# One change to a decoder-trunk kernel: the two ends of the up projection, own buffers for one load of the down projection, and 32 bytes reserved in SBUF

## The chip, the cores and the metric

The kernel runs on one core of a Trainium2 chip. The metric is the device time of one execution in microseconds (us), the median of the runs shown. TensorE (PE) does the matrix products and transposes, VectorE (DVE) and ScalarE (ACT) the elementwise work, GpSimd (POOL) and SyncE (SP) here mostly start transfers between the chip's memory and SBUF, the on-chip memory of 128 partitions from which the engines read. Products are collected in PSUM, in eight banks of 512 float32 columns.

## The reference, cut to what matters

Three sub-layers stand one behind the other, each with a norm ahead of it, a norm behind it and a residual: a mixer (pooling and forgetting attention, joined by gates), attention to 256 memory tokens, and a gated MLP. The change lies in the last, apart from the reserved bytes, which concern all. S is 1024, D_MODEL 1024, D_FF 2816.

```python
def conv_ffn(h, w_up, conv_w, conv_b, w_down):
    z = h @ w_up
    zc = conv_w[2] * z + conv_w[1] * shift_right(z, 1) + conv_w[0] * shift_right(z, 2) + conv_b
    g, u = zc[..., :D_FF], zc[..., D_FF:]
    return (jax.nn.gelu(g, approximate=True) * u) @ w_down
...
        x = x + rms_norm(merged @ w_mix_out[l], mix_post_g[l])
...
        x = x + rms_norm(mem_attention(h, mem_n, w_xq[l], w_xkv[l], w_xo[l]), xa_post_g[l])
        h = rms_norm(x, ffn_pre_g[l])
        x = x + rms_norm(conv_ffn(h, w_up[l], conv_w[l], conv_b[l], w_down[l]), ffn_post_g[l])
```

## The kernel before

**Products of three matmuls.** Every float32 operand is split into a high part (a copy on ACT, rounded to the matmul's type) and a low part (source minus high, on DVE); `split` does both, on L101 and L102. A product is high times high, high times low and low times high. A matmul holds 128x128 of one operand (the stationary one, the second of its two names in the profile) and streams the other (the moving one, the first name) through it, nearly always 512 columns.

**Two sides of SBUF.** Tile pools take their space from the left end or from the right end. On the left lie `const`, `sm` and `ap` (28 slots of 4 KB a partition with tag A, given out by `slot`), on the right, up to the down projection, `hp` (four large operands, `hslot`) and `wp` (split weights), and from then on `dp` (`dslot`). As the program is built, tiles on the left begin at multiples of 64 bytes, and tiles on the right at 32 bytes above a multiple of 64, since the right end of the space given out, 229344, is itself 32 above one.

**Up projection.** For each of 22 pairs of column blocks (j), seven products p1 to p7 (`product_up`, 12 matmuls each, L1105) take the place of eight, on sums of operand blocks. `up_steps` is the order of these 154 products, n its index. Moving operands: b11, b21, t3 and t4 lie in `hp`, t1, t2 and b22 in `ap` slots. Stationary operands rotate through six pairs (`up_ops`): four pairs `wh`/`wl` in `wp` on the right, two `ox` on the left. `z` collects the results (ACT copies and DVE additions out of PSUM); `gate_done` and `pair_done` convolve, apply the gelu, multiply and store.

**Its start.** The tokens' last quarter (q4 = 3) is transposed on PE (`xtrans(3)`, L915) ahead of product n = 4, through PSUM banks that `ring(q=(0, 1))` gives out, two in turn; ACT copies them out (L918, into `xr`). The sums t1 to t4 of quarters 2 and 3 come from the generator `b_sums`; `plan` says after which product which of its steps is written. The t4 step of quarter 2 consists of two DVE operations on `tr` (L1055, L1056) and a split into `t`.

**Its end.** Product 153 is p4 of j = 21. Behind the loop stand the loads (`load`) and the splits (`prepare`) of the first HEAD = 4 steps of the down projection: their raw data goes into the up projection's raw slots (`head_raw`), their operands into the slots of t1 and t2 (`head_ops`).

**Down projection.** Steps (p, k), seven products by eleven k, 12 matmuls each (L1287). `load(i + 4)` and `prepare(i + 2)` are written ahead of `products(i)`. Weights of products other than p1 go through a ring of four buffers, `wd`. For p7, each pair of steps loads two of them, b22 and b12, DVE subtracts the second from the first in place (L1255), and the difference is split.

The loads on SP keep their written order. Otherwise a scheduler of the framework sets the order on each engine, so that the written order is only its starting point.

Of the kernel before, what the change touches and what calls it, by code (L numbers as in the profile page):

```python
# [9 lines left out]
F32 = mybir.dt.float32  # L10
# [6 lines left out]
P = 128  # L17
# [7 lines left out]
NJ = FF // P  # L25
# [13 lines left out]
def hybrid_kernel(ctx, tc, out, x, xT, g_col, mem, gains, b_forget, w_fm, w_v0, w_v1, pool_w, pool_scale,  # L39
                  w_pool_br, w_fox_br, w_mix_out, w_xq, w_xk, w_xv, w_xo, w_up, conv_w, conv_b,  # L40
                  w_down):
    nc = tc.nc
    const = ctx.enter_context(tc.tile_pool(name="const", bufs=1))
    sm = ctx.enter_context(tc.tile_pool(name="sm", bufs=16))
    ap = ctx.enter_context(tc.tile_pool(name="ap", bufs=28))

    front = ctx.enter_context(ExitStack())
    hp = front.enter_context(tc.tile_pool(name="hp", bufs=4, side="right"))
# [26 lines left out]
    def ring(**kinds):  # L75

        rings.clear()
        for k, ids in kinds.items():
            rings[k] = [list(ids), 0]
# [404 lines left out]
    def step(gen, n):  # L484
        for _ in range(n):
            next(gen, None)
# [118 lines left out]
    t1 = [slot(s="t1") for _ in range(8)]  # L605
# [290 lines left out]
    def xtrans(q4, k2s=range(4)):  # L896

        for n in ("b11", "b21"):
            if n not in quarters:
                quarters[n] = hslot(n)  # L900
        if q4 >= 2 and q4 not in raws_b:
            raws_b[q4] = ([slot((P, 4, 256), s="rb") for _ in range(2)] if q4 == 2 else
                          [t.rearrange("p (k n) -> p k n", k=4) for t in xrs[q4]])
        c = slice((q4 % 2) * 256, (q4 % 2) * 256 + 256)
        if q4 < 2:
            def dst(k2):
                o, k = quarters[("b11", "b21")[k2 // 2]], 2 * (k2 % 2)
                return o[:, k:k + 2, c], o[:, 4 + k:6 + k, c]
            transpose_pair(yrs[q4], dst, k2s, g_cols[:, 2])
            return  # L910
        for k2 in k2s:
            b = bank("q").rearrange("p (k t) -> p k t", k=2)
            for kk in range(2):
                for t in range(2):
                    nc.tensor.transpose(b[:, kk, t * P:(t + 1) * P],  # L915
                                        yrs[q4][t][:, (2 * k2 + kk) * P:(2 * k2 + kk + 1) * P], ident)
            for kk in range(2):
                nc.scalar.activation(raws_b[q4][k2 // 2][:, 2 * (k2 % 2) + kk], b[:, kk], AF.Copy,  # L918
                                     scale=g_cols[:, 2, 2 * k2 + kk:2 * k2 + kk + 1])
# [117 lines left out]
    def b_sums(q4):  # L1037

        c = slice((q4 % 2) * 256, (q4 % 2) * 256 + 256)
        r12, r22 = raws_b[q4]  # L1040
        t_ = slot((P, 4, 256), s="tr") if q4 == 2 else g_post.rearrange("p (k n) -> p k n", k=4)
        b11, b21 = quarters["b11"], quarters["b21"]
        nc.vector.tensor_tensor(t_, r12, f32(b11[:, :4, c]), ALU.subtract)
        nc.vector.tensor_tensor(t_, t_, f32(b11[:, 4:, c]), ALU.subtract)
        b_split(q4, "t1", t_)
        yield
        nc.vector.tensor_tensor(t_, r22, t_, ALU.subtract)
        b_split(q4, "t2", t_)
        yield
        b_split(q4, "b22", r22)  # L1050
        yield
        nc.vector.tensor_tensor(r12, r22, r12, ALU.subtract)
        b_split(q4, "t3", r12)
        yield
        nc.vector.tensor_tensor(t_, f32(b21[:, :4, c]), t_, ALU.subtract)  # L1055
        nc.vector.tensor_tensor(t_, t_, f32(b21[:, 4:, c]), ALU.add)  # L1056
        b_split(q4, "t4", t_)
        yield
# [24 lines left out]
    ps = psum.enter_context(tc.tile_pool(name="ps2", bufs=1, space=bass.MemoryType.PSUM, reuse_waits="tile"))  # L1083
    eight = [ps.tile([P, 512], F32, tag=f"c{i}", name=f"acc{i}", bufs=1) for i in range(8)]
    banks[:] = eight[4:]
    ring(q=(0, 1))
    UX, UZ, UY = [eight[i] for i in (6, 0, 2, 7)], [eight[i] for i in (1, 3)], eight[4:6]
    up_raws += yrs[2]
    up_ops += [tuple(o[:, i].rearrange("p k n -> p (k n)") for i in range(2)) for o in ox]
# [7 lines left out]
    def product_up(n):  # L1097
        j, p = up_steps[n]
        o = {"p5": UY[j % 2], "p3": UY[j % 2], "p2": UZ[j % 2]}.get(p, UX[j % 4])
        ah, al = operand_up.pop(n)  # L1100
        bh, bl = b_part(B_OF[p], 0), b_part(B_OF[p], 1)
        for k in range(4):
            ks = slice(k * P, (k + 1) * P)
            for i, (l, r) in enumerate(((ah, bh), (ah, bl), (al, bh))):
                nc.tensor.matmul(o, l[:, ks], r[k // 2][:, k % 2], start=i == k == 0 and p in ("p1", "p5", "p2"),  # L1105
                                 stop=i == 2 and k == 3, skip_group_check=True)
        if p == "p1":
            z[j] = [slot(s="zg"), None]
            nc.scalar.activation(z[j][0][:, left], o, AF.Copy)
        elif p == "p5":  # L1110
            z[j][1] = slot(s="zu")
            nc.scalar.activation(z[j][1][:, right], o, AF.Copy)
        elif p == "p6":
            nc.scalar.activation(z[j][0][:, right], o, AF.Copy)
        elif p == "p3":
            nc.vector.tensor_add(z[j][0][:, right], z[j][0][:, right], o)
        elif p == "p7":
            nc.vector.tensor_add(z[j][1][:, right], z[j][1][:, right], o)
        elif p == "p2":
            nc.vector.tensor_add(z[j][0][:, left], z[j][0][:, left], o)  # L1120
        else:
            nc.scalar.activation(z[j][1][:, left], o, AF.Copy)
# [11 lines left out]
    def gate_done(j):  # L1134
        gates[j] = conv_wide(z[j][0], j)
        nc.scalar.activation(gates[j], gates[j], AF.Gelu_apprx_tanh)

    def pair_done(j):

        d = conv_wide(z[j][1], NJ + j)  # L1140
        nc.vector.tensor_mul(d, d, gates.pop(j))
        nc.gpsimd.dma_start(out=act_d[j], in_=d)
        z.pop(j)
        act_ring[j] = d
        if j % 2:
            s_ = slot((P, 512), s="sd")
            nc.vector.tensor_tensor(s_, act_ring.pop(j - 1)[:, right], act_ring.pop(j)[:, right], ALU.add)
            nc.gpsimd.dma_start(out=sum_d[j // 2], in_=s_)

    sums_b3[3] = b_sums(3)  # L1150

    plan = {0: ((2, 1),), 1: ((2, 1),), 2: ((2, 1),), 3: ((2, 1),), 4: ((3, 1),), 5: ((3, 2),), 6: ((3, 1),), 7: ((3, 1),)}
    done_up = set()
    waiting = []
    for n in range(len(up_steps)):
        j, p = up_steps[n]
        if n == 4:
            xtrans(3)
        product_up(n)
        for q4, m in plan.get(n, ()):  # L1160
            step(sums_b3[q4], m)
        prepare_up()

        while waiting and waiting[0][0] <= n:
            waiting.pop(0)[1]()
        done_up.add((j, p))
        defer = 4 if j < 6 else 0
        for jj in (j - 1, j):
            if (jj, "g") not in done_up and {(jj, "p3"), (jj, "p2")} <= done_up:
                done_up.add((jj, "g"))  # L1170
                waiting.append((n + defer, lambda jj=jj: gate_done(jj)))
        if p == "p4":
            waiting.append((n + defer, lambda j=j: pair_done(j)))

    HEAD = 4
    front.close()  # L1180
    dp = ctx.enter_context(tc.tile_pool(name="dp", bufs=6, side="right", reuse_waits="tile"))

    def dslot(tag, dt=F32, bufs=None):
        return dp.tile([P, 2, 512], dt, tag=tag, name=nm(tag), bufs=bufs)

# [9 lines left out]
    operands = {}  # L1195
    got = {}

    head_raw = [t.rearrange("p (k n) -> p k n", k=2) for t in up_raws[2:]]
    head_ops = [t for n in ("t1", "t2") for half in range(2) for t in b_slots[n, half]]

    LOADS = {"p1": ("a11", "b11"), "p5": ("s", "b12"), "p6": ("b22", "a12"), "p3": ("b22", "a21"),
             "p7": ("b22", "b12"), "p2": ("b21",), "p4": ("a22",)}
# [2 lines left out]
    def load(i):  # L1205

        p, k = steps[i]
        if k % 2:
            return
        n = min(2, NK - k)  # L1210

        def send(out, in_):
            in_order(nc.sync.dma_start(out=out, in_=in_))

        for q in LOADS[p]:
            if q == "s":
                r = dslot("sa")
                for kk in range(n):
                    send(r[:, kk], sum_d[k + kk])
            elif q[0] == "a":  # L1220
                r = head_raw.pop(0) if i < HEAD else slot((P, 2, 512), s=q)
                c = slice((int(q[1]) - 1) * 512, int(q[1]) * 512)
                for kk in range(n):
                    send(r[:, kk], act_d[2 * (k + kk) + int(q[2]) - 1][:, c])
            else:
                r = (dslot("wd", bufs=4) if p != "p1" else head_raw.pop(0) if k < HEAD else
                     dslot("sb"))
                c = slice((int(q[2]) - 1) * 512, int(q[2]) * 512)
                send(r[:, :n], w_pairs[int(q[1]) - 1][:, k:k + n, c])
            got[q if q in ("a11", "a12", "s") else (p, q), k // 2] = r  # L1230
# [45 lines left out]
                    got.pop(((p, q), k2))  # L1276

    accs = {"x": eight[:4], "y": eight[4:]}

    def products(i, ts=range(4)):  # L1280
        p, k = steps[i]
# [56 lines left out]
            eng.dma_start(out=out[tg * P:(tg + 1) * P, ns], in_=xt[:, ns])  # L1338

    AHEAD = 2  # L1340
    for i in range(HEAD):
        load(i)
    for i in range(HEAD):
        prepare(i)
    for i in range(len(steps)):
        p, k = steps[i]
        if i + 2 * AHEAD < len(steps):
# [93 lines left out]
```

## Time and profile before

| | us |
|---|---|
| median of 3 runs | 1515.12 |
| lowest and highest run | 1515.02, 1515.87 |
| the profiled execution | 1518.38 |
| its span | 1516.6 |
| PE busy | 1466.8 |
| DVE busy | 1024.3 |
| ACT busy | 715.8 |

The mean granted clock of the profiled execution is 0.989 of full speed. The span runs from about 0 to 1516.6: the mixer to about 609 us, its output projection to about 700, the attention to 855, the up projection to 1284, the down projection from there. In the timeline rows the first number is the start and the second the length of a group of equal instructions, and the bracket says how long the engine was idle before it and what released it. Successive matmuls overlap by their drain, so that the distance of two starts, not the duration of one, is what a matmul costs in a row of matmuls.

### The profile page before, as it was taken

To read this page: it belongs to the slowest core of one execution; us is meant where nothing else is said; L and a number is where in the kernel's file an instruction comes from. 1 tells how busy PE (TensorE), PEld (TensorE's weight loads), DVE (VectorE), ACT (ScalarE), POOL (GpSimd) and SP (SyncE) were. 2 spreads that over 40 slices of the span, in tenths; PEclk is the share of its full clock that TensorE was granted. 3 is DMA by queue.
4 is the path that set the end of the run, shared out by engine and by line. 5 is a ranking of instruction groups with operands and counts; after the bars stand their busy time and mean duration, and the time that the engine had idled before them with its cause. 6 is when DMAs were issued, how large, how long until landed. Compare 5 with 4: busy or idle time off the path is not lost. (4 is left out here: it accounts for less than half of the span.)

```text
span 1516.6 us, 19098 instructions
## 1 busy us (share of the span) xinstructions
PE 1466.8 (97%) x7052; PEld 1211.5 (80%) x7052; DVE 1024.3 (68%) x1505; ACT 715.8 (47%) x1328; POOL 135.5 (9%) x303
## 2 busy tenths in 40 slices
PE   7999999999999999999999799999999998999996
PEld 7988888778888888877788588888888887888785
DVE  7578787673234344576646789787778876786785
ACT  6355655322222233455668755454444444444362
POOL 4101000000000000042112100000000000000003
PEclk9999999999999999999999899999999999999998
DMA  5254343111111224344412223222222223863542
GB/s 170 70 124 96 81 107 76 43 42 48 50 61 43 84 80 158 110 142 164 139 56 98 97 70 118 91 76 91 91 90 91 91 91 120 287 217 98 185 149 111
DMA packets 62014, 159.49 MB, mean 105 GB/s; under 512 B 7585, under 2 KB 8033, under 8 KB 61921
## 3 DMA queue, kind: packets, MB, share of 16 engines
q1 hardware_dynamic: 49472, 114.20, 25.3%
q0 software_dynamic: 12304, 43.82, 8.0%
q8 instruction: 55, 0.90, 0.3%
q14 instruction: 39, 0.31, 0.1%
q10 hardware_dynamic: 144, 0.26, 0.0%
HBM read 118.50 MB, written 27.16 MB: 96 GB/s over the span
## 5 line engine op out<-in xcount | busy, mean ns | idle before, releaser
L101 ACT ACTIVATE wh<-wr 128x512 fp32r<-128x512 f32 x137 | 85.3, 628 | 225.9 <-PE wide L234 124.1
L1287 PE MATMUL acc<-o,o 128*128 128x512 f32 x828 | 188.9, 390 | 1.8 <-DVE o L102 1.8
L1287 PEld LDWEIGHTS acc<-o,o 128*128 128x128 f32 x828 | 155.1, 188 | 35.5 <-DVE o L102 3.3
L1105 PE MATMUL acc<-t,wh 128*128 128x512 f32 x472 | 147.1, 393 | 0.0
L102 DVE TENSOR_TENSOR wl<-wr,wh 128x512 fp32r<-128x512 f32 x137 | 93.0, 686 | 61.1 <-ACT wh L101 61.0
L1105 PE MATMUL acc<-b,wh 128*128 128x512 f32 x360 | 111.8, 392 | 0.0
L1105 PEld LDWEIGHTS acc<-t,wh 128*128 128x128 f32 x472 | 88.6, 188 | 20.1
L1105 PE MATMUL acc<-t,wl 128*128 128x512 f32 x236 | 92.7, 393 | 0.0
L1105 PE MATMUL acc<-t,ox 128*128 128x512 f32 x348 | 84.0, 393 | 0.0
L236 PE MATMUL wide<-h,wl 128*128 128x512 f32 x256 | 79.5, 390 | 1.0 <-DVE wl L102 1.0
L232 PE MATMUL wide<-h,wh 128*128 128x512 f32 x256 | 79.5, 391 | 0.5 <-ACT wh L101 0.3
L1105 PEld LDWEIGHTS acc<-b,wh 128*128 128x128 f32 x360 | 67.5, 188 | 14.8
L234 PE MATMUL wide<-h,wh 128*128 128x512 f32 x256 | 79.1, 390 | 0.0
L163 PE MATMUL bank<-h,wh 128*128 128x512 f32 x192 | 77.0, 401 | 1.5 <-DVE qk L441 1.5
L101 ACT ACTIVATE wh<-su 128x512 fp32r<-128x512 f32 x59 | 37.1, 630 | 86.5 <-DVE su L1008 52.4
L1105 PEld LDWEIGHTS acc<-t,ox 128*128 128x128 f32 x348 | 65.3, 188 | 15.1
L164 PE MATMUL bank<-h,wh 128*128 128x512 f32 x192 | 75.9, 396 | 0.0
L165 PE MATMUL bank<-h,wl 128*128 128x512 f32 x192 | 75.7, 394 | 0.0
L1105 PE MATMUL acc<-b,wl 128*128 128x512 f32 x180 | 70.5, 392 | 0.0
L1105 PE MATMUL acc<-b,ox 128*128 128x512 f32 x252 | 63.7, 404 | 0.0
L613 DVE TENSOR_TENSOR sg<-wide,r1b 128x1024 f32<-128x1024 f32 x16 | 19.6, 1224 | 62.7 <-PE wide L236 62.7
L102 DVE TENSOR_TENSOR pt<-bank,pt 128x512 fp32r<-128x512 f32 (+2 forms) x96 | 50.9, 551 | 11.0 <-ACT pt L101 10.7
(387 smaller groups left out, 3545.2 us busy)
## 6 DMA issues: line engine op xcount, KB each, us to landing
wd<-in_w_down SPq DMA_DIRECT2D x30, 512.0 KB
wr<-in_w_fm SPq DMA_DIRECT2D x28, 512.0 KB
act<-d POOLq DMA_DIRECT2D x22, 512.0 KB, 2.9
a<-act SPq DMA_DIRECT2D x40, 256.0 KB
wr<-in_w_mix_out SPq DMA_DIRECT2D x16, 512.0 KB
wr<-in_w_up SPq DMA_DIRECT2D x16, 512.0 KB
ur<-in_w_up SPq DMA_DIRECT2D x14, 512.0 KB
y<-in_w_up SPq DMA_DIRECT2D x14, 512.0 KB
```

What stands on the lines that cost most here:

```text
L101: nc.scalar.activation(hi, src, AF.Copy)
L102: nc.vector.tensor_tensor(lo, src, f32(hi), ALU.subtract)
L163: nc.tensor.matmul(o, lh, rh, start=start, stop=False)
L164: nc.tensor.matmul(o, lh, rl, start=False, stop=False)
L165: nc.tensor.matmul(o, ll, rh, start=False, stop=stop)
L232: nc.tensor.matmul(o[h], wh[:, ks], hT[h][0][:, k], start=st, stop=False)
L234: nc.tensor.matmul(o[h], wh[:, ks], hT[h][1][:, k], start=False, stop=False)
L236: nc.tensor.matmul(o[h], wl[:, ks], hT[h][0][:, k], start=False, stop=sp)
L613: nc.vector.tensor_mul(sg, og, r1b)
L1105: nc.tensor.matmul(o, l[:, ks], r[k // 2][:, k % 2], start=i == k == 0 and p in ("p1", "p5", "p2"), stop=i == 2 and k == 3, skip_group_che ...
L1287: nc.tensor.matmul(o, oa[:, l, tt], ob[:, r], start=n == k == 0 and p in ("p1", "p5", "p2"), stop=n == 2 and k == NK - 1, skip_group_check ...
```

## The change

Four things are done.

- A tile of 32 bytes a partition is taken from the right end first, and zeroed by one POOL instruction. As built, all tiles of the right pools that a matmul reads then begin at multiples of 64 bytes, as on the left.
- At the start of the up projection the transposes' ring has three banks, (3, 0, 1), and the t4 step of quarter 2 is written after product 7 and no longer after product 3.
- At its end the loads of the first four down steps are written after p3 of j = 21, and their splits after p7 (steps 0 and 1) and p2 (steps 2 and 3); the gate and the convolutions of j = 21 go to the list `later`, from which the down projection takes one entry a step.
- The b12 tiles of p7 get `ap` slots of their own (`wd7`) instead of buffers of the ring `wd`.

```diff
     ap = ctx.enter_context(tc.tile_pool(name="ap", bufs=28))
+
+    pad = ctx.enter_context(tc.tile_pool(name="pad", bufs=1, side="right"))
+    nc.gpsimd.memset(pad.tile([P, 8], F32, name="pad"), 0.0)
...
-    ring(q=(0, 1))
+    ring(q=(3, 0, 1))
...
-    plan = {0: ((2, 1),), 1: ((2, 1),), 2: ((2, 1),), 3: ((2, 1),), 4: ((3, 1),), 5: ((3, 2),), 6: ((3, 1),), 7: ((3, 1),)}
+    plan = {0: ((2, 1),), 1: ((2, 1),), 2: ((2, 1),), 4: ((3, 1),), 5: ((3, 2),), 6: ((3, 1),), 7: ((2, 1), (3, 1))}
...
         product_up(n)
+        if (j, p) == (NJ - 1, "p3"):
+            head_raw += [t.rearrange("p (k n) -> p k n", k=2) for t in up_raws[2:]]
+            head_ops += [t for n_ in ("t1", "t2") for half in range(2) for t in b_slots[n_, half]]
+            for i in range(HEAD):
+                load(i)
+        for i in {"p7": (0, 1), "p2": (2, 3)}.get(p, ()) if j == NJ - 1 else ():
+            prepare(i)
...
-        defer = 4 if j < 6 else 0
+        defer = 4 if j < 6 else 0 if j < NJ - 1 else 99
...
-                r = (dslot("wd", bufs=4) if p != "p1" else head_raw.pop(0) if k < HEAD else
+                r = (dslot("wd", bufs=4) if (p, q) not in (("p1", "b11"), ("p7", "b12")) else
+                     slot((P, 2, 512), s="wd7") if p == "p7" else head_raw.pop(0) if k < HEAD else
                      dslot("sb"))
...
-    for i in range(HEAD):
-        load(i)
-    for i in range(HEAD):
-        prepare(i)
```

Apart from these lines, definitions move ahead of the loop, and line numbers shift: up to about L1150 a line of before is three further down in the changed kernel.

**ACT at the start of the up projection.** The rows begin with the copy of product n = 3's result. `t_853` before and `t_855` afterwards are the operand t4, `tr` its source, `xr` the transposed last quarter. Before:

```order
L1109 ACTIVATE zg_7230<-acc_7127 128x512
L101 ACTIVATE t_853_7255<-tr_7090 128x2x256 x2
L918 ACTIVATE xr_7000<-acc_7131,g_cols 128x256 x2
L918 ACTIVATE xr_7000<-acc_7132,g_cols 128x256 x2
L918 ACTIVATE xr_7001<-acc_7131,g_cols 128x256 x2
L101 ACTIVATE b_847_7208<-xr_7001 128x2x256
L918 ACTIVATE xr_7001<-acc_7132,g_cols 128x256 x2
```

Afterwards:

```order
L1112 ACTIVATE zg_7235<-acc_7132 128x512
L104 ACTIVATE t_855_7369<-tr_7095 128x2x256 x2
L921 ACTIVATE xr_7005<-acc_7139,g_cols 128x256 x2
L921 ACTIVATE xr_7005<-acc_7136,g_cols 128x256 x2
L921 ACTIVATE xr_7006<-acc_7137,g_cols 128x256 x2
L921 ACTIVATE xr_7006<-acc_7139,g_cols 128x256 x2
L104 ACTIVATE b_847_7213<-xr_7006 128x2x256
```

The split of t4 stays ahead of the first copy of a transposed block; the four pairs of copies now stand together, and three banks take the place of two.

**DVE at the same place.** `wl_6080` before, `wl_6085` afterwards, is the low part of a stationary operand of product n = 7. Before:

```order
L1120 TENSOR_TENSOR zg_7182<-zg_7182,acc_7128 128x512
L102 TENSOR_TENSOR b_849_7210<-rb_7059,b_847_7208 128x2x256
L1055 TENSOR_TENSOR tr_7090<-b_775_6688,tr_7090 128x1024
L102 TENSOR_TENSOR b_850_7211<-rb_7059,b_848_7209 128x2x256
L1056 TENSOR_TENSOR tr_7090<-tr_7090,b_775_6688 128x1024
L102 TENSOR_TENSOR wl_6080<-y_6786,wh_6079 128x512
L102 TENSOR_TENSOR t_853_7255<-tr_7090,t_853_7255 128x2x256
```

Afterwards:

```order
L1123 TENSOR_TENSOR zg_7187<-zg_7187,acc_7133 128x512
L105 TENSOR_TENSOR b_849_7215<-rb_7064,b_847_7213 128x2x256
L105 TENSOR_TENSOR wl_6085<-y_6791,wh_6084 128x512
L105 TENSOR_TENSOR b_850_7216<-rb_7064,b_848_7214 128x2x256
L1058 TENSOR_TENSOR tr_7095<-b_775_6693,tr_7095 128x1024
L1059 TENSOR_TENSOR tr_7095<-tr_7095,b_775_6693 128x1024
L1123 TENSOR_TENSOR zg_7235<-zg_7235,acc_7135 128x512
```

The low part `wl` moved from behind the two operations on `tr` to a place ahead of them.

**ACT at the end of the up projection.** `ur` and `y` are the raw slots with the first down operands, `t_832` to `t_835` and `t_843` to `t_846` the operand slots, `zu` and `zg` copies out of PSUM. Before:

```order
L1122 ACTIVATE zu_9781<-acc_7133 128x512
L1136 ACTIVATE d_9873<-d_9873 128x1024
L1112 ACTIVATE zu_9906<-acc_7132 128x512
L1127 ACTIVATE d_9910<-zu_9781,cbt,cwt 128x1024
L1114 ACTIVATE zg_9868<-acc_7127 128x512
L1127 ACTIVATE d_9983<-zg_9868,cbt,cwt 128x1024
L1122 ACTIVATE zu_9906<-acc_7127 128x512
L1136 ACTIVATE d_9983<-d_9983 128x1024
L101 ACTIVATE t_832_7093<-ur_6987 128x512
L101 ACTIVATE t_834_7095<-ur_6987 128x512
```

Afterwards:

```order
L1125 ACTIVATE zu_9786<-acc_7138 128x512
L104 ACTIVATE t_832_7098<-ur_6992 128x512
L104 ACTIVATE t_834_7100<-ur_6992 128x512
L104 ACTIVATE t_835_7101<-ur_6994 128x512
L104 ACTIVATE t_833_7099<-ur_6994 128x512
L1139 ACTIVATE d_9878<-d_9878 128x1024
L1115 ACTIVATE zu_9911<-acc_7137 128x512
L1130 ACTIVATE d_9915<-zu_9786,cbt,cwt 128x1024
L1117 ACTIVATE zg_9873<-acc_7132 128x512
L104 ACTIVATE t_843_7190<-y_6790 128x512
L104 ACTIVATE t_844_7191<-y_6791 128x512
L104 ACTIVATE t_845_7192<-y_6790 128x512
```

Four splits now stand ahead of a gelu and of the copy of p5's result (`zu_9911`), four more (three are shown) ahead of the copy of p4's, which was row seven before.

**PE at the same place**, the last rows of the up projection and the first of the down projection. Before:

```order
L1105 MATMUL acc0_7127<-t4_853_7255,wh_692_6083 128x512 x2
L1105 MATMUL acc0_7127<-t4_853_7255,wl_693_6084 128x512
L1287 MATMUL acc0_7127<-t1_833_7094,t1_832_7093 128x512 x3
L1287 MATMUL acc1_7128<-t1_833_7094,t1_832_7093 128x512 x3
L1287 MATMUL acc2_7129<-t1_833_7094,t1_832_7093 128x512 x3
L1287 MATMUL acc3_7130<-t1_833_7094,t1_832_7093 128x512 x3
```

Afterwards:

```order
L1108 MATMUL acc0_7132<-t4_855_7369,wh_692_6088 128x512 x2
L1108 MATMUL acc0_7132<-t4_855_7369,wl_693_6089 128x512
L1298 MATMUL acc1_7133<-t1_833_7099,t1_832_7098 128x512 x3
L1298 MATMUL acc2_7134<-t1_833_7099,t1_832_7098 128x512
L1298 MATMUL acc0_7132<-t1_833_7099,t1_832_7098 128x512 x3
L1298 MATMUL acc2_7134<-t1_833_7099,t1_832_7098 128x512 x2
L1298 MATMUL acc3_7135<-t1_833_7099,t1_832_7098 128x512 x3
```

Four matmuls of the first down step moved ahead of those into bank acc0, from which p4's result has to be copied first.

**SP at p7's loads**, with the semaphores that each load waits for. Before:

```order
L1213 DMA wd_10890<-in_w_down 128x2x512 [waits DMAHW2_49,DVE_49]
L1213 DMA wd_10892<-in_w_down 128x2x512 [waits DMAHW3_49,DVE_49]
L1213 DMA wd_10932<-in_w_down 128x2x512 [waits DMAHW4_49,DMAHW3_49,DVE_49]
L1213 DMA wd_10934<-in_w_down 128x2x512 [waits DMAHW5_49,DVE_49]
L1213 DMA wd_10973<-in_w_down 128x2x512 [waits DMAHW6_49,DMAHW0_49,DVE_49]
```

Afterwards:

```order
L1187 DMA wd_10895<-in_w_down 128x2x512 [waits DMAHW2_49,DVE_49]
L1187 DMA wd_1084_10897<-in_w_down 128x2x512 [waits DMAHW3_49]
L1187 DMA wd_10937<-in_w_down 128x2x512 [waits DMAHW4_49,DVE_49]
L1187 DMA wd_1090_10939<-in_w_down 128x2x512 [waits DMAHW5_49]
L1187 DMA wd_10978<-in_w_down 128x2x512 [waits DMAHW6_49,DVE_49]
```

The order of the loads is the same; every second one (`wd_1084`, `wd_1090`) no longer waits for DVE.

## Rows read from the trace of the kernel before

**Rows 1.** The page, part 1: busy time, share, instructions of each engine

```profile
PE 1466.8 (97%) x7052; PEld 1211.5 (80%) x7052; DVE 1024.3 (68%) x1505; ACT 715.8 (47%) x1328; POOL 135.5 (9%) x303
```

**Rows 2.** PE's waits, whole span: line, releaser, total us, times, longest

```profile
PE acc L915 <- ACT xr L918: 7.4, 1, 7.4
...
PE acc L1287 <- ACT t L101: 4.7, 1, 4.7
```

**Rows 3.** Windows: us, busy of PE, PEld, DVE, ACT, POOL, clock, DMA share, GB/s

```profile
610.00:660.00 50.00, 50.00 (x216) 40.18 (x215) 29.93 (x47) 25.90 (x53) 2.47 (x7) 1.00 0.28 93
...
1320.00:1370.00 50.00, 50.00 (x222) 41.42 (x221) 43.68 (x57) 25.08 (x45) 0.00 (x0) 1.00 0.61 204
```

**Rows 4.** Timeline of PE, up projection: start, length, engine, line, operation, tiles, count

```profile
968.74 5.75 PE L1105 MATMUL acc<-b,ox 128*128 128x512 f32 x24
...
1267.15 5.63 PE L1105 MATMUL acc<-t,ox 128*128 128x512 f32 x24
1272.62 0.62 PE L1105 MATMUL acc<-b,wh 128*128 128x512 f32 x2
...
1274.71 0.63 PE L1105 MATMUL acc<-b,wh 128*128 128x512 f32 x2
```

**Rows 5.** Timeline of PE at the start of the up projection

```profile
865.60 1.12 PE L915 MATMUL acc<-ident,y 128*128 128x128 f32 x4 [7.38 <-ACT xr L918]
```

**Rows 6.** Timeline of ACT at the same place

```profile
863.67 1.15 ACT L101 ACTIVATE t<-tr 128x512 fp32r<-128x512 f32 x2 [2.87 <-DVE tr L1056]
864.73 1.55 ACT L918 ACTIVATE xr<-acc,g_cols 128x256 f32<-128x256 f32 x4
```

**Rows 7.** Timeline of DVE at the same place

```profile
862.42 1.22 DVE L1056 TENSOR_TENSOR tr<-tr,b 128x1024 f32<-128x1024 f32 x1
863.55 0.68 DVE L102 TENSOR_TENSOR wl<-y,wh 128x512 fp32r<-128x512 f32 x1
```

**Rows 8.** Window behind that wait, columns as in rows 3

```profile
868.00:872.00 4.00, 4.00 (x12) 3.24 (x12) 3.29 (x5) 2.52 (x6) 0.00 (x0) 0.56 0.00 0
```

**Rows 9.** Timeline of PE where the up projection ends

```profile
1283.35 0.39 PE L1105 MATMUL acc<-t,wl 128*128 128x512 f32 x1
1288.42 14.40 PE L1287 MATMUL acc<-t,t 128*128 128x512 f32 x48 [4.68 <-ACT t L101]
1302.67 1.54 PE L1287 MATMUL acc<-o,o 128*128 128x512 f32 x6
```

**Rows 10.** Timeline of ACT there

```profile
1267.70 0.58 ACT L1122 ACTIVATE zu<-acc 128x512 f32<-128x512 f32 x1
...
1270.81 0.58 ACT L1112 ACTIVATE zu<-acc 128x512 f32<-128x512 f32 x1
...
1283.78 0.60 ACT L1122 ACTIVATE zu<-acc 128x512 f32<-128x512 f32 x1 [0.75 <-PE acc L1105]
...
1286.72 2.17 ACT L101 ACTIVATE t<-ur 128x512 fp32r<-128x512 f32 x4
```

**Rows 11.** Windows there: before the wait on ACT, and behind it

```profile
1268.00:1284.00 16.00, 15.74 (x70) 12.61 (x68) 9.06 (x10) 5.02 (x7) 0.53 (x1) 1.00 0.27 98
...
1290.00:1292.00 2.00, 2.00 (x6) 1.56 (x5) 1.88 (x3) 2.00 (x4) 0.00 (x0) 0.50 0.99 376
```

**Rows 12.** Timeline of PE in p7 of the down projection

```profile
1417.64 13.93 PE L1287 MATMUL acc<-o,o 128*128 128x512 f32 x60 [0.32 <-DVE o L102]
1431.90 5.74 PE L1287 MATMUL acc<-o,o 128*128 128x512 f32 x24 [0.33 <-DVE o L102]
1438.78 11.54 PE L1287 MATMUL acc<-o,o 128*128 128x512 f32 x49 [1.14 <-DVE o L102]
```

**Rows 13.** DVE's waits from 1380 to 1450, columns as in rows 2

```profile
DVE wd L1255 <- DMA wd<-in_w_down: 8.8, 6, 2.1
```

**Rows 14.** Timeline of PE in the mixer's attention, scores of one block

```profile
121.77 0.39 PE L458 MATMUL wide<-kd,qs 128*128 128x512 f32 x1
...
122.47 0.40 PE L459 MATMUL wide<-ke,qe 68*128 68x512 f32 x1
```

More of the change, by code (lines that the diff above doesn't have):

```diff
@@ L1148, in pair_done @@
             nc.gpsimd.dma_start(out=sum_d[j // 2], in_=s_)
-    sums_b3[3] = b_sums(3)
-    plan = {0: ((2, 1),), 1: ((2, 1),), 2: ((2, 1),), 3: ((2, 1),), 4: ((3, 1),), 5: ((3, 2),), 6: ((3, 1),), 7: ((3, 1),)}
[L1153 to L1166, printed above, removed]
-        defer = 4 if j < 6 else 0
[L1168 to L1173, printed above, removed]
     HEAD = 4
-    front.close()
-    dp = ctx.enter_context(tc.tile_pool(name="dp", bufs=6, side="right", reuse_waits="tile"))
     def dslot(tag, dt=F32, bufs=None):
@@ L1196, in hybrid_kernel @@
     got = {}
-    head_raw = [t.rearrange("p (k n) -> p k n", k=2) for t in up_raws[2:]]
-    head_ops = [t for n in ("t1", "t2") for half in range(2) for t in b_slots[n, half]]
+    head_raw, head_ops = [], []
     LOADS = {"p1": ("a11", "b11"), "p5": ("s", "b12"), "p6": ("b22", "a12"), "p3": ("b22", "a21"),
@@ L1278, in hybrid_kernel @@
     accs = {"x": eight[:4], "y": eight[4:]}
+    sums_b3[3] = b_sums(3)
+    plan = {0: ((2, 1),), 1: ((2, 1),), 2: ((2, 1),), 4: ((3, 1),), 5: ((3, 2),), 6: ((3, 1),), 7: ((2, 1), (3, 1))}
+    done_up = set()
+    waiting = []
+    for n in range(len(up_steps)):
+        j, p = up_steps[n]
+        if n == 4:
+            xtrans(3)
+        product_up(n)
+        if (j, p) == (NJ - 1, "p3"):
[5 more added lines that the diff above has]
+            prepare(i)
+        for q4, m in plan.get(n, ()):
+            step(sums_b3[q4], m)
+        prepare_up()
+        while waiting and waiting[0][0] <= n:
+            waiting.pop(0)[1]()
+        done_up.add((j, p))
+        defer = 4 if j < 6 else 0 if j < NJ - 1 else 99
+        for jj in (j - 1, j):
+            if (jj, "g") not in done_up and {(jj, "p3"), (jj, "p2")} <= done_up:
+                done_up.add((jj, "g"))
+                waiting.append((n + defer, lambda jj=jj: gate_done(jj)))
+        if p == "p4":
+            waiting.append((n + defer, lambda j=j: pair_done(j)))
+    front.close()
+    dp = ctx.enter_context(tc.tile_pool(name="dp", bufs=6, side="right", reuse_waits="tile"))
     def products(i, ts=range(4)):
```

## The prediction

> **What bounds the kernel now.** First the page's busy times: PE works 1466.8 of 1516.6 us [rows 1], so the time is PE's idle time, 49.8 us, and what a matmul costs while PE is busy. Second PE's waits: the longest single one, 7.4 us on ACT's `xr`, stands at the start of the up projection, and one of 4.7 us on ACT's `t` at its end [rows 2]. Third, how fast a busy PE works. Two stretches of 50 us, both without idle time and at clock 1.00, hold 216 and 222 matmuls of 512 columns [rows 3]. A stretch counts each that touches it, so its length and one matmul's 0.39 us, divided by the count, is the distance of two starts: 50.39/216 = 233 ns and 50.39/222 = 227 ns. That is 2.8% with the same instruction.
>
> What distinguishes them is where the operands lie. The first stretch streams split weights from the right (`wh`, `wl`) against tiles on the left, the second has both on the right. In the up projection, 24 `b,ox` (moving from the right, stationary on the left) take 5.75 us, (5.75 - 0.39)/23 = 233 ns from start to start; 24 `t,ox`, both on the left, take 1272.62 - 1267.15 = 5.47 us, 228 each; behind them nine `b,wh` and `b,wl`, `b` being b22 on the left and `wh` on the right, take 1274.71 - 1272.62 = 2.09 us, 232 each [rows 4]. So both on one side is fast, on either side, and one on each is slow, in either direction. I read this as alignment: right tiles begin 32 bytes above a multiple of 64, left tiles at one. A boundary of some SBUF half does not fit as well: left tiles lie on both sides of the middle of the space and behave alike.
>
> **The change part by part**, against the profiled execution's 1518.4 us.
>
> *The 32 bytes.* I went through all matmuls of 512 columns, took the addresses of the moving tile and of the next stationary one (the one that is loaded meanwhile) from the built program, and the distance of starts from the trace. 2044 undisturbed pairs are mixed (the `b,ox` and `b,wh` of [rows 4] are among the last), by 6.3 ns over 227.0 on average, which is also the difference in [rows 3]: 2044 x 6.3 = 12.9 us. Some 2.6 us of it lie ahead of 540, 2.9 in 540 to 700, 1.8 in 700 to 850, 5.5 in the up projection, nothing in the down projection. The pad makes all of them equal. Where PE waits for others soon after, some of the gain is eaten: ahead of the 7.4 us wait PE's own results feed ACT and DVE, so a chain that starts earlier also ends earlier, and I take off only 0.6. Term **-12.3**. Bounds: -14.5, if the some 80 pairs left out as disturbed and the slow matmuls just behind a change of side gain as well; 0, if alignment is not the cause. POOL's added instruction is its first, and nobody there waits for it.
>
> A page of the Trainium skill speaks against this: "TensorE: Matmul & The Clock Gate", section "Step-by-step: what each phase is for", says that PE has two independent read ports, so that loading the next weights takes no SBUF bandwidth from the running matmul. By it the place of the stationary tile could not matter, the pad's term would be nothing, and the sum that of the second rival below. The trace does not agree as it stands, 233 against 227 ns by where the next stationary tile lies; but that it is the address's last six bits, and not the side, no run here shows yet.
>
> *The start.* PE resumes at 865.60 [rows 5] when ACT has made its first copy into `xr`. ACT did not wait for PE's transposes there but stood behind the split of t4, which waited 2.87 us for DVE's L1056 [rows 6]; DVE ended that at 863.64 [rows 7]. Writing that split behind product 7 should take it out of the way; the order as built shows that it does not: t4's split still stands ahead of all `xr` copies. Worse, `wl`, 0.68 us long [rows 7], moves from behind L1056 to ahead of it, so that L1056 and with it PE's wait end some 0.7 later. For it: three banks let PE do 12 of the 16 transposes ahead of the wait and not 8, so four fewer stand behind it; four there took 1.12 us, a product's first matmul beside them [rows 5]. PE runs at half clock behind the wait, 0.56 in 868 to 872 [rows 8], as it will again. Set row against row, the end of product n = 4 comes 0.3 later, and 0.1 is added for a stationary operand of a later product (n = 11) whose low part is ready that much after it is wanted. Term **+0.4**; bounds -1 (the four transposes for nothing and `wl` hidden, 1.12 at most) and +1.5 (`wl` twice over, 1.36).
>
> *The end.* Before, PE ends its last up matmul's turn at 1283.35 + 0.23, starts again at 1288.42, and does the next 48 matmuls in 14.25 us until 1302.67 [rows 9], most of them at half clock, 0.50 in 1290 to 1292 [rows 11]. The loads had long come; the splits waited behind p4's evacuation and a gelu on ACT, 1283.78 to 1286.72 [rows 10]. Afterwards four splits stand right behind ACT's copy of 1267.70, where ACT is idle for 11 of 16 us [rows 11]; they wait until p5 has read t1 (its 12 matmuls end at about 1269.9) and take 2.17 us [rows 10], until 1271.0. DVE's eight low parts, 0.68 each [rows 7], 5.4 us, go into 6.9 idle us of the same stretch [rows 11]. So PE goes on: 48 x 0.227 = 10.9 us from 1283.58, to 1294.5 and not 1302.7: **-8.2** (4.8 of idle time, 3.4 of half clock). Its cover is thin at two places. The copy of p5 (L1112, before at 1270.81) comes behind splits and gelu at some 1272.5, and p3 wants to add into that bank at 1272.62 [rows 4]; it may cost 0 to 0.3. And p4's copy ends at 1284.38 [rows 10], when PE has done four matmuls into other banks, 1283.58 + 0.91 = 1284.49. If either misses, it costs tenths; if both do and the second step's splits are late too, 2 us: bounds -8.6 and -6. The gate of j = 21, which is late instead, feeds only loads for the last k.
>
> *p7's own buffers.* PE waits 0.32, 0.33 and 1.14 us for DVE's `o` [rows 12], DVE 8.8 us in six times for loads into `wd` [rows 13], and those loads wait until DVE has freed the ring. From 1417.64 to 1438.78 PE needs 21.14 us for 84 matmuls, 84 x 0.227 = 19.07; with the 0.32 ahead that is 2.4 too many. Afterwards every second load waits for no DVE, and the ring holds twice as many steps of the others. Term **-2.3**; bounds -2.7, and +0.5, if earlier weights hold up a load behind them on SP, one of the waits in [rows 12] doubled.
>
> Sum: 1518.4 - 12.3 + 0.4 - 8.2 - 2.3 = 1496.0. The profiled execution lies 3.3 above the median of 1515.12, so the forecast is **1492.7**.
>
> **The rivals.**
> Half of the alignment gain is eaten: what PE gains ahead of 855 (2.6 + 2.9 + 1.8 = 7.3) goes into its waits there. For it: 49.8 us of idle time, most of it ahead of the up projection. Against it: those waits follow from PE's own earlier results. 1492.7 + 6.7 = 1499.4.
> Alignment is not the cause, and left and right differ by their place in SBUF: the pad moves tiles by 32 bytes and no more, and gives nothing. 1492.7 + 12.3 = **1505.0**. For it: in before, side and alignment go together in every pair. Against it: mixed pairs are slow in both directions, and left tiles behave alike wherever they lie.
> Slower: not equality is fast but the 32-byte offset, and the 2803 pairs with both on the right, fast now, become as slow as mixed ones, while mixed ones stay: 2803 x 6.3 = 17.7 in the place of -12.3, 1492.7 + 30.0 = 1522.7. For it: in the mixer's attention scores, with all operands on the left, three distances take 0.70 us, 233 ns each [rows 14]. Against it: the `t,ox` at 228 [rows 4], also on the left, and that those scores stand in groups of four between waits. It turns the sign once equal pairs cost over 231 ns after the change (10.1 us of other terms over 2803 pairs is 3.6 ns above 227).
> The change does not do what it says: at the start that is the forecast already; at the end it would be the splits staying behind the gelu, +8.2, 1500.9; the order as built speaks against it.
>
> **How the numbers follow.** Forecast 0.70; eaten 0.08; no alignment 0.15; slower 0.03; the end's gain missing 0.04. The forecast's own bounds are 1518.4 - 3.3 - 14.5 - 8.6 - 2.7 - 1.0 = 1488.3 and, with the milder ends (-10 for the pad), about 1499. The range 1488.5 to 1505.5 takes in the eaten gain, the missing end and half of "no alignment", about 0.83 in all. A measurement of this kernel tells 0.2%, 3 us, from no change. All cases but one lie below 1512: faster 0.95, within 0.015, slower 0.035.
>
> **What would show it.** Pad: 24 `b,ox` in 5.45 us, 222 matmuls in 50 us of the mixer's output projection. Start: PE's wait on `xr` still there, 7 to 8 us. End: no wait on `t`, clock 1.00 through 1284 to 1300. p7: DVE's wait at its subtraction under 3 us. Wrong would be a mixed pair still at 233 ns, or PE idle for over 1 us at the end of the up projection.

## The result and the profile after

The changed kernel takes 1498.01 us (median of 4 runs, 1495.82 to 1499.68) against 1515.30: ratio 0.9885, 95% interval 0.9867 to 0.9902, faster by 17.3 us. Forecast were 1492.7, 5.3 lower than measured, and a range of 1488.5 to 1505.5. Two later series of the same kernel, each beside the kernel before, gave 1492.51 (0.9859, interval 0.9839 to 0.9878) and 1496.96 (0.9873, 0.9857 to 0.9890); one of the four executions of the first series was disturbed (3747.86 us) and is left out. The profiled execution took 1495.82 us, 22.6 less than that of before; the sum of the terms was 22.4.

The page, part 1, of the changed kernel, and below it PE's waits (line, releaser, total us, times, longest):

```profile
PE 1449.2 (97%) x7052; PEld 1209.0 (81%) x7052; DVE 1022.6 (68%) x1505; ACT 714.1 (48%) x1328; POOL 134.9 (9%) x304
```

```profile
PE acc L918 <- ACT xr L921: 7.9, 1, 7.9
...
PE acc L1298 <- DVE o L105: 0.4, 1, 0.4
```

PE's busy time fell by 17.6 us from [rows 1] with the same 7052 instructions: most of the gain is that the same work takes less time. Of the waits of [rows 2], the one on `t` at the end of the up projection is gone, the one on `xr` is there still and 0.5 longer.

Windows of the changed kernel, columns as in [rows 3]; the first stretch is the one that held 216 matmuls before:

```profile
610.00:660.00 50.00, 50.00 (x222) 41.44 (x221) 31.33 (x47) 27.01 (x54) 5.34 (x10) 1.00 0.32 105
1300.00:1350.00 50.00, 50.00 (x222) 41.42 (x221) 44.24 (x58) 24.51 (x44) 0.00 (x0) 1.00 0.59 200
```

Both stretches now hold 222. PE's timeline in the up projection and at its end:

```profile
961.07 5.60 PE L1108 MATMUL acc<-b,ox 128*128 128x512 f32 x24
...
1254.83 5.60 PE L1108 MATMUL acc<-t,ox 128*128 128x512 f32 x24
1260.27 0.62 PE L1108 MATMUL acc<-b,wh 128*128 128x512 f32 x2
...
1262.31 0.62 PE L1108 MATMUL acc<-b,wh 128*128 128x512 f32 x2
...
1271.15 11.13 PE L1298 MATMUL acc<-t,t 128*128 128x512 f32 x48
1282.11 23.06 PE L1298 MATMUL acc<-o,o 128*128 128x512 f32 x101
```

The 24 `b,ox` of [rows 4] took 5.75 us and take 5.60, (5.60 - 0.39)/23 = 226.5 ns each (the prediction's sign, 5.45, is 24 distances and leaves out that this length holds 23 and one matmul's 0.39, together 5.61); the nine matmuls between the two `b,wh` rows take 2.04 us and not 2.09. Behind the up projection there is no idle time and no half clock: 48 matmuls in 10.96 us, where [rows 9] had 4.68 of idle time and 14.25.

ACT there, with its eight splits in idle time (`ur` and `y` are the raw slots):

```profile
1255.86 2.18 ACT L104 ACTIVATE t<-ur 128x512 fp32r<-128x512 f32 x4
...
1258.89 0.58 ACT L1115 ACTIVATE zu<-acc 128x512 f32<-128x512 f32 x1
...
1260.98 2.19 ACT L104 ACTIVATE t<-y 128x512 fp32r<-128x512 f32 x4
1271.35 0.60 ACT L1125 ACTIVATE zu<-acc 128x512 f32<-128x512 f32 x1 [8.18 <-PE acc L1108]
```

Both thin covers held: p5's copy (L1115) ends at some 1259.5, and p3 starts at 1260.27; p4's copy ends by 1271.95, and PE comes to its bank after four matmuls, at 1271.15 + 0.91.

### The profile page after: what moved, and what is told of

Read it like the earlier page. It is cut to its first block, busy times and chain, and to the rows that moved or that the text cites. A ratio compares the mean times of both kernels' runs of the same rounds, so it can differ in the third digit from the quotient of the medians.

```text
span 1493.7 us, 19105 instructions
## 1 busy us (share of the span) xinstructions
PE 1449.2 (97%) x7052; PEld 1209.0 (81%) x7052; DVE 1022.6 (68%) x1505; ACT 714.1 (48%) x1328; POOL 134.9 (9%) x304
## 4 chain that ended last, share of the span: by engine, by line
PE 83%; DVE 5%; DMA 5%; ACT 2%; issue 2%; POOL 2%; SPq 0%; DVEq 0%; ACTq 0%; POOLq 0%
PE acc L1108 28%; PE acc L1298 10%; PE bank L166 6%; PE bank L167 6%; PE bank L168 6%; PE wide L235 4%; PE wide L239 4%; PE wide L237 4%; PE bank L557 3%; PE wide L166 3%; PE wide L167 3%; PE wide L168 2%; DMA wd<-in_w_down 2%; PE bank L546 2%; DVE o L105 1%
```

## The experiments

The table sets every profiled kernel against the profiled execution of before, in us, by stretches of PE's matmuls in their order, counted from 0 to 7051: ahead of the first up product (0 to 4250), the wait and product n = 4 (4316 to 4346), the up projection behind it (4346 to 6010), its end (6010 to 6160), and from the middle of p7 to the last matmul (6610 to 7051). What lies between stays within 0.3.

| kernel | ahead | start | up | end | p7 on | all |
|---|---|---|---|---|---|---|
| changed | -5.4 | -0.9 | -6.2 | -8.3 | -2.2 | -22.9 |
| changed, again (e9) | -4.6 | -0.6 | -6.2 | -8.3 | -0.3 | -19.8 |
| pad only (e1) | -5.9 | -0.6 | -6.3 | -0.7 | -1.1 | -14.4 |
| no pad (e2) | -1.0 | -0.4 | 0.0 | -8.1 | -0.9 | -10.4 |
| left end too (e3) | -7.3 | -0.4 | -6.2 | -0.5 | -0.9 | -15.4 |
| left 64 lower (e4) | -2.9 | -1.0 | -0.9 | -8.1 | -2.3 | -14.8 |
| left 128 lower (e8) | -3.7 | 0.5 | 0.0 | -8.1 | -2.7 | -14.0 |
| left 256 lower (e12) | -6.5 | 0.5 | -6.2 | -8.3 | 0.4 | -20.1 |
| start undone (e10) | -6.2 | -0.8 | -6.2 | -8.3 | -2.6 | -24.0 |
| ring for p7 (e11) | -5.8 | 0.5 | -6.2 | -8.3 | -0.1 | -19.9 |
| late t4 (e6) | -7.7 | -4.7 | -4.6 | -8.3 | -1.6 | -26.7 |
| late t4, p2 own (e7) | -8.0 | -4.6 | -4.7 | -8.3 | -1.4 | -27.0 |

### Is it alignment?

e1 is the kernel before with the pad alone:

```diff
+    pad = ctx.enter_context(tc.tile_pool(name="pad", bufs=1, side="right"))
+    nc.gpsimd.memset(pad.tile([P, 8], F32, name="pad"), 0.0)
```

> The kernel before with the 32 bytes at the right end and nothing else of the change. Theory A (a matmul of 512 columns costs 227 ns where its moving tile and the next stationary tile begin at the same address modulo 64, and 233 where they don't): 11 to 12 us faster, about 1503.8; the 24 b,ox at 227 ns; the three waits of the start, the end and p7 unchanged. Theory B (left and right side of SBUF, not alignment): no change, 1515.3, the 24 b,ox still at 233.

1504.28 us, ratio 0.9916 (0.9902 to 0.9930): 12.6 faster.

e2 is the changed kernel with these two lines taken out.

> The changed kernel without the 32 bytes. Theory A: what the three other edits give alone, by the changed kernel's trace 8.3 (end) + 2.2 (p7) + 0.7 (start) = 11.2, so about 1504; mixed pairs back at 233 ns. Theory B: as the changed kernel, 1498.

1506.29 us, 0.9931 (0.9916 to 0.9946): 10.6 faster, 2.3 slower than expected, mixed pairs at 233 ns again.

e3 leaves the right end alone and shifts the left:

```diff
+    padl = ctx.enter_context(tc.tile_pool(name="padl", bufs=1))
+    nc.gpsimd.memset(padl.tile([P, 8], F32, name="padl"), 0.0)
     const = ctx.enter_context(tc.tile_pool(name="const", bufs=1))
```

> The kernel before with 32 bytes taken at the left end in the place of the right: all operands of both sides begin 32 above a multiple of 64. Theory A (equal remainders): the same gain as with 32 bytes on the right, 11 to 12 us, about 1503.8. Theory C (multiples of 64 are fast for themselves): nothing gained, and the 2803 pairs with both on the right stay at 227, those on the left get slower, 1515 to 1518. Theory B: 1515.3.

1503.52 us, 0.9911 (0.9898 to 0.9925): the same gain, with everything 32 bytes off a multiple of 64.

e4, e8 and e12 are the changed kernel with the left pools' large tiles lower by 64, 128 and 256 bytes, by smaller constants (e4) and by fewer buffers for the smallest tiles:

```diff
-        return sm.tile([P, cols], F32, tag=f"s{cols}", name=nm(s))
+        return sm.tile([P, cols], F32, tag=f"s{cols}", name=nm(s), bufs=12)
```

This is e12; e8 has it for one of the two sizes. PE, DVE and ACT have the changed kernel's order in both.

> The changed kernel with the left pools' tiles 64 bytes lower (three small constants share two tiles): left and right are equal modulo 64 and differ by 64 modulo 128. If the granule is 64 bytes: as the changed kernel, 1498, mixed pairs at 227. If it is 128 bytes: the 11.6 us are lost again, about 1509.6, mixed pairs at 233.

> The changed kernel with the left pools' big tiles 128 bytes lower (twelve instead of sixteen buffers for the smallest tiles): left and right equal modulo 128, differing by 128 modulo 256. If 128 bytes is the granule: mixed pairs at 227 ns, about 1498. If it is 256 or more: 230 to 233 ns in mixed pairs, as with 64 bytes, about 1506.

> The changed kernel with the left pools' big tiles 256 bytes lower (twelve buffers for both sizes of smallest tiles): equal modulo 256, different modulo 512. Differences of 32, 64 and 128 bytes gave 233 ns in mixed pairs; if the granule is 256 bytes, 227 and about 1496; if it is 512, the length of one row of a stationary tile, 230 to 233 and about 1505.

1505.94 (0.9926, 0.9911 to 0.9941) for 64 bytes; one execution each for 128, 1504.72, and 256, 1498.60. The same group of 24 `b,ox` (right moving, left stationary) in PE's timelines of e2, e3, e4, e8 and e12, in this order:

```profile
967.47 5.75 PE L1105 MATMUL acc<-b,ox 128*128 128x512 f32 x24
```

```profile
959.44 5.60 PE L1107 MATMUL acc<-b,ox 128*128 128x512 f32 x24
```

```profile
964.97 5.66 PE L1109 MATMUL acc<-b,ox 128*128 128x512 f32 x24
```

```profile
965.58 5.75 PE L1108 MATMUL acc<-b,ox 128*128 128x512 f32 x24
```

```profile
961.18 5.60 PE L1108 MATMUL acc<-b,ox 128*128 128x512 f32 x24
```

Equality is what counts, not the multiple (e3 is as fast as e1), and equality modulo 256 bytes: with a difference of 32 (e2) or 128 (e8) a matmul costs 233 ns, with 64 (e4) 229 to 233, by the pair, and 256 (e12) costs nothing. The column "up" says the same over 1664 matmuls: -6.2 or -6.3 in every kernel with equal remainders (but e6 and e7, which wait there, see below), 0.0 with 32 and 128, -0.9 with 64. The rival by which the pad gives nothing falls, and so does the slower one: the pairs on the right stay at 227. The four scores of [rows 14], 233 ns apart before, lie 237 apart in the changed kernel:

```profile
122.15 0.39 PE L461 MATMUL wide<-kd,qs 128*128 128x512 f32 x1
...
122.86 0.40 PE L462 MATMUL wide<-ke,qe 68*128 68x512 f32 x1
```

So they were no evidence on the offset. What slows them was not tried, nor which of the two stationary tiles beside a matmul, its own or the next, has to match. The trace of before says something on the second at the ends of up products (from n = 12 on), where the two lie on different sides. With moving and own tile on one side and the next on the other, a matmul takes 235 ns (23 cases); with moving and next on the right and its own on the left, 229 to 230 (13). That speaks for the next one; but with moving and next on the left and its own on the right it takes 236 (10), so that it stays open.

### The start

e9 is the changed kernel once more, e10 has the old ring and the old plan:

```diff
-    ring(q=(3, 0, 1))
+    ring(q=(0, 1))
...
-    plan = {0: ((2, 1),), 1: ((2, 1),), 2: ((2, 1),), 4: ((3, 1),), 5: ((3, 2),), 6: ((3, 1),), 7: ((2, 1), (3, 1))}
+    plan = {0: ((2, 1),), 1: ((2, 1),), 2: ((2, 1),), 3: ((2, 1),), 4: ((3, 1),), 5: ((3, 2),), 6: ((3, 1),), 7: ((3, 1),)}
```

> The changed kernel once more, for a second profile beside the next two. Expected: median 1493 to 1498; 227 ns in mixed pairs; no wait of PE at the end of the up projection. At its start PE's wait of 7.9 us on xr again, but the time at half clock behind it anywhere from 2.9 us (first profile) to 5.6 us (the run with left tiles 128 bytes lower, whose instructions stand in the same order).

> The changed kernel with the ring of two banks and the old plan for the sums. If the start's edit has a gain of its own: product n = 4 ends 0.7 us later against the matmuls ahead of it than in the changed kernel, and 0.7 in the median. If the 0.7 of the first profile was the clock coming back earlier in that execution: PE resumes some 0.8 us after fewer transposes as forecast (wait 7.2 to 7.5), and the end of n = 4 differs from the changed kernel's by what its time at half clock differs by; the medians within 1 us of each other.

e10 took 1495.62 us (0.9871, 0.9856 to 0.9886), e9 1496.96: no difference beyond the intervals. PE at this place in the changed kernel, in e10 and in e11, which has the changed kernel's order here:

```profile
861.15 1.12 PE L918 MATMUL acc<-ident,y 128*128 128x128 f32 x4 [7.91 <-ACT xr L921]
861.92 6.47 PE L1108 MATMUL acc<-b,ox 128*128 128x512 f32 x23
```

```profile
859.58 1.12 PE L918 MATMUL acc<-ident,y 128*128 128x128 f32 x4 [7.38 <-ACT xr L921]
```

```profile
860.56 1.12 PE L918 MATMUL acc<-ident,y 128*128 128x128 f32 x4 [7.91 <-ACT xr L921]
861.33 7.95 PE L1108 MATMUL acc<-b,ox 128*128 128x512 f32 x23
```

The same 23 matmuls take 6.47 us in one execution and 7.95 in the other. The clock (last column but two) says why; windows of the changed kernel, then of e11:

```profile
860.00:864.00 4.00, 2.85 (x9) 2.46 (x10) 3.29 (x4) 4.00 (x11) 0.00 (x0) 0.50 0.00 0
864.00:868.00 4.00, 4.00 (x18) 3.26 (x18) 3.30 (x6) 2.08 (x4) 0.00 (x0) 1.00 0.00 0
```

```profile
860.00:864.00 4.00, 3.44 (x10) 2.91 (x11) 3.28 (x4) 3.95 (x11) 0.00 (x0) 0.50 0.00 0
864.00:868.00 4.00, 4.00 (x14) 3.14 (x13) 2.00 (x4) 1.54 (x3) 0.00 (x0) 0.68 0.00 0
```

PE resumes 0.6 us later in the changed kernel, and yet is at full clock by 864, while in e11 the half clock goes on past it. The column "start" runs from -1.0 to 0.5 among the seven kernels with the same order there, with 2.8 to 6.0 us between PE's resuming and the clock's return, and e10, with the old order, lies inside at -0.8. That PE waits 7.4 us with the old order and 7.9 with the edit is what e10's second case expected.

e6 does what the edit could not: a written order that the scheduler keeps holds ACT's split of t4 behind the copies into `xr`.

```diff
+                if q4 == 3:
+                    in_order(act)
...
+            if q4 == 2 and name == "t4":
+                in_order(nc.scalar.activation(hi[i][:, :, c], src[:, 2 * i:2 * i + 2], AF.Copy))
```

> The changed kernel with t4's split of quarter 2 held behind the copies of xr in ACT's order. Theory (the wait of 7.9 us on xr is ACT's order, behind a split that waits for DVE): PE's wait falls to some 3 us, product n = 4 ends 4 to 5 us earlier, 1498 becomes about 1494. Rival (DVE, busy without a break from 852 to 867, sets the pace of the start anyway): the wait falls, but as much is waited for t1's low parts before product n = 8, and the time stays within 1 us of the changed kernel's.

1492.35 us, 0.9851 (0.9836 to 0.9866). The timeline of PE:

```profile
853.96 1.11 PE L918 MATMUL acc<-ident,y 128*128 128x128 f32 x4 [3.39 <-ACT xr L921]
854.73 7.42 PE L1114 MATMUL acc<-b,ox 128*128 128x512 f32 x24
...
876.86 0.73 PE L1114 MATMUL acc<-t,ox 128*128 128x512 f32 x2 [1.12 <-ACT ox L104]
```

The wait falls from 7.9 to 3.4 and the stretch by some 4 us: it was ACT's order. At 876.86 PE then waits for an operand that DVE and ACT prepare, and the column "up" loses 1.6 of it. So both theories hold in part. The net gain of 2.2 to 2.5 us in these two columns is 0.2 in the medians (1492.51 beside it), inside the intervals: not shown as a gain in time.

### p7

e11 puts p7's b12 back in the ring of the changed kernel; e7 is e6 with own slots for p2's loads as well:

```diff
-                r = (dslot("wd", bufs=4) if (p, q) not in (("p1", "b11"), ("p7", "b12")) else
+                r = (dslot("wd", bufs=4) if p != "p1" or q != "b11" else
```

```diff
-                     slot((P, 2, 512), s="wd7") if p == "p7" else head_raw.pop(0) if k < HEAD else
+                     slot((P, 2, 512), s="wd7") if p in ("p7", "p2") else head_raw.pop(0) if k < HEAD else
```

> The changed kernel with p7's b12 back in the ring of four. If own slots bring 2.2 us there: from the first down matmuls to the last the trace takes 2.2 us longer than the changed kernel's, with three waits of PE on o in p7 as before. If the waits depend on how PE meets the loads and not on the slots: 0 to 1 us, as in the kernel before with the pad alone, which lost less there than the kernel before.

> As the run with t4's split late, and p2's b21 tiles get own slots as p7's b12 have. The changed kernel gives 0.65 us of p7's gain back in p2, where DVE waits for loads into wd: if these wait for the ring, another 0.6 us and no wait of PE in p2; if for the transfers themselves, no change.

e11: 1498.44 us (0.9880, 0.9863 to 0.9897); e7: 1492.03 (0.9851, 0.9833 to 0.9869), as e6. DVE's waits for loads from 1365 to 1450 in the changed kernel and in e11:

```profile
DVE sb L1248 <- DMA wd<-in_w_down: 6.7, 6, 2.5
...
DVE wd L1230 <- DMA wd<-in_w_down: 3.8, 2, 2.1
```

```profile
DVE wd L1230 <- DMA wd<-in_w_down: 8.5, 5, 2.2
...
DVE sb L1248 <- DMA wd<-in_w_down: 4.4, 4, 1.4
```

In these two profiles own slots take 4.7 us off the waits at p7's subtraction (L1230), and 2.3 come back at p2's (L1248); in e9 the two waits are 5.9 and 6.9. The prediction's sign, under 3 us at p7's subtraction, did not come. What reaches PE differs between executions of one kernel; PE's waits in the down projection in e9 and in e11:

```profile
PE acc L1298 <- DVE o L105: 1.4, 3, 0.5
```

```profile
PE acc L1298 <- DVE o L105: 1.6, 2, 1.2
```

e9, with own slots, waits nearly as long as e11 without, and the changed kernel's first profile 0.4. In all, PE waits 1.1 to 1.8 us for these operands in the four profiles with the ring, and 0 to 2.1 (e12) in the eight with own slots for p7 alone. Over those eight the last stretch takes 100.2 to 103.3 us, mean 101.3; over the four 101.8 to 102.8, mean 102.3. About 1 us, of which no single pair of runs is proof. With p2's loads in own slots as well (e7) it took 101.4: no further gain.

### The spread

> The changed kernel once more, beside the kernel before, to see how far its executions and two profiles of it spread. If only the spread of single executions lies between the 22.8 us that the two traces differ by and the 17.3 of the medians: a ratio of 0.986 to 0.988, and a trace that agrees with the first from product n = 4 on within 0.5 us, with differences ahead of that. If the first profile was a lucky one in a stage that the change touches: a difference of 2 us or more in the end of the up projection or in p7.

e5 gave the 1492.51 above; the second profile is e9's. It agrees with the first within 0.1 in the up projection and its end, and differs by 0.8 ahead, 0.4 at the start and 2.0 from p7 on. So the 3.1 us between these two executions, as much as the spread of 3 to 4 us in a series, come from the places where PE waits for others, not from those where it works. Why the three medians lie 5.5 us apart, no run settles.

## Why the prediction was right, and where not

**The 32 bytes: mechanism right, size too large.** Forecast -12.3, of which 5.5 in the up projection and 7.3 ahead, less 0.6. The up projection gave 6.2 (some 0.7 more, since the pairs that were counted as fast gained too: both on the left from 228.2 to 226.7 ns, 230 of them, both on the right from 227.3 to 226.7, 622). Ahead, the nine profiles with equal remainders lie at -4.6 to -8.0, mean -6.4, the four without at 0 to -3.7, mean -1.9: 4.5 of 7.3. The step that was off is the 7.3 with "I take off only 0.6": some 2.8 are missing there. Only in part is that waiting: compared one by one (medians of the nine and of before, e2 and e8), the undisturbed matmuls of 512 columns gain 5.7 and not 7.3, and PE's idle time there is 0.5 longer (mean of the nine 15.8, of the four 15.3). The rest stays open. In all -10.7, from profiles; the timed gains of equal remainders alone, 12.6 (e1) and 13.4 (e3), show no shortfall, though in the profile of e1 p7 too happened to be 1.1 shorter, and in that of e3 0.9. That row and rule differ stands: TensorE: Matmul & The Clock Gate, a page of the Trainium skill, section "Step-by-step: what each phase is for", says that loading the next weights takes no SBUF read bandwidth from the running matmul; e2, e3, e8 and e12 show 6 ns a matmul by nothing but the remainder of its operands' addresses.

**The end: right.** Forecast -8.2, and -8.3 in every kernel that has it with equal remainders; -8.1 without. Cover and clock came as described. The splits did not wait until p5 had read t1, as the prediction says: the first began at 1255.86, 1.0 us after p5 at 1254.83. Its sum there was off too, since 1269.9 and 2.17 are 1272.1 and not 1271.0; the splits' early start made up for it.

**The start: right for the order, wrong for the clock.** That t4's split would stay ahead, and that PE would resume later, came true: against the work ahead of it PE resumes 0.9 us later (861.15, with 5.36 gained by then, against 865.60), 0.7 were forecast. The term of +0.4 rested on "half clock ... as it will again", taken as just as long; it lasts from 2.8 to 6.0 us in profiles with one order, which is worth up to 1.5 us. In the three in which it lasted 5.9 to 6.0, against 5.9 before (e8, e11, e12), the column shows +0.5: the order's own cost was forecast well. The bounds, -1 to +1.5, held. The same page of the Trainium skill, section "What's actually happening", says that the chip's look at activity runs freely, so that one kernel meets it differently from run to run; the two executions of 6.47 and 7.95 us agree.

**p7: too large, and what is late next was missing.** Forecast -2.3; single profiles gave -2.7 to +0.4, about -1 on average against the mean of those with the ring. PE's waits recur with the ring, but own slots do not end them in every execution, as the term of 2.3 supposed; and p2's subtraction, which then waits for loads instead, was not named, though it stands a few lines behind in the code.

**From the profile to the median.** The sum, 22.4, against the profiled pair's 22.6 looks exact, and is partly luck: with the sizes above it is 10.7 + 8.3 + 1.0 = 20, beside 17.3, 18.8 and 23.5 in the three series of medians. The 3.3 us by which the profiled execution of before lay above its median were taken off as if they belonged to both kernels. The table says that this execution was long ahead of the up projection, by 1 to 4 us against the three others whose mixed pairs are slow. A gain read from its long places is in part a gain against that one execution.

What e1 and e2 gain in the medians, 12.6 + 10.6 = 23.2, is more than two of the three series of the whole change and as much as the third; no run settles it. The chances over the range, 0.70 + 0.08 + 0.04 and half of 0.15, add up to 0.90, not 0.83.

## What to carry to other kernels

Where PE is the bound, compare what equal matmuls cost in different stretches before looking for waits: 2.8% of a matmul is seen in a count of matmuls per window, and in no list of waits. For matmuls like these, the tiles that are read together should begin at equal addresses modulo 256 bytes, which two pools that grow from both ends need not give. A write order that a scheduler may change is no order: look at the built order, and pin what matters (e6 got at the start what two edits of the written order did not).

## What the runs showed of the hardware

A matmul of 512 float32 columns takes 226.5 to 227 ns from start to start at full clock when its moving tile and the stationary tiles beside it begin equal modulo 256 bytes, and 233 when they differ by 32 or 128; with 64 it takes 229 to 233. Equal pairs of the up projection that stand between unequal ones take a little longer, 227.3 and 228.2 in before. It makes no difference whether that common remainder is a multiple of 64 (e1) or not (e3).

After a wait of 7.9 us PE ran at half clock for 2.8 us in one execution (861.15 to about 864) and for 6.0 in another (860.56 to about 866.6: a mean clock of 0.68 in 864 to 868), with the same instructions there in the same order.
